# Gate blocks copied to DRAM in runs of 16 KB, the first three copies of a set issued late, and 48 parked score blocks in place of 44

## The chip, the cores and the metric

The kernel runs on one core of one Trainium2 chip. The time is the device time of one execution in microseconds (us). TensorE (PE) multiplies matrices, VectorE (DVE) and ScalarE (ACT) work elementwise, GpSimd (POOL) issues the gathers of single rows here, SyncE (SP) issues most loads. DMA queues started by SP, ACT and POOL share 16 DMA engines.

## The reference

One decoder layer on 512 tokens of width 2048: attention and a recurrent branch, then a retrieval layer with 16384 experts of one neuron each. The change touches only the last part:

```python
s1 = jnp.einsum('chd,hnd->chn', q[:, :, 0], keys1); s2 = ...   # 8 heads, 128 keys each
v1, i1 = lax.top_k(s1, 16); v2, i2 = lax.top_k(s2, 16)
top, pos = lax.top_k(v1[..., :, None] + v2[..., None, :], 16)  # 16 of 256 pairs
e = i1[pos // 16] * 128 + i2[pos % 16]                         # expert numbers
g = jax.nn.softmax(top, axis=-1)
act = jax.nn.gelu(einsum('chkd,cd->chk', u_tab[e], x))
out = einsum('chk,chkd->cd', g * act, v_tab[e])
```

## The kernel before

The first 960 us or so (projections, attention, recurrent branch, output projection, queries and the choice of the top 16) are untouched. Then the retrieval layer splits the tokens. For the first 160 tokens the rows of the two expert tables are gathered one by one: one row for each token (1 MB) per gather, started by POOL (`gather`, L932) into one of a few row buffers, and one product on DVE (L953, L959 or L965) per gather. One such product with its gather is a **side step** (`side`); there are 320. For the other 352 tokens (`TD`) the kernel computes the scores of all experts densely, in 128 **blocks** of 128 experts.

One block is an **S job**: two halves of weights (`ud`), each loaded by SP into a `raw` buffer (L135; both halves are one load of 1 MB), split by ACT into a rounded part `hi` (L152) and by DVE into a rest `lo` (L153), and multiplied by PE in 48 matmuls (L197 to L199, 24 for each half). Four pairs of `hi` and `lo` exist. The result goes through Gelu (L753 or L1130) and is multiplied by the block's **gate** matrix `G`. Four blocks make a group; the output products of a group are four **V jobs** (48 matmuls each, L1154 to L1156).

The gates come from one-hot products. DVE makes one-hot matrices for four tokens at a time (`onehots`, L998 to L1001), PE multiplies them (12 small matmuls, `gate_mm`, L1014), ACT copies the result from PSUM into the staging tile `stg` (L1016). After eight such steps, a **set** of 32 tokens, `stg` holds 2 MB and ACT starts its copy to the DRAM tensor `GD` (L1019). There are 11 sets and one `stg`, so the first copy of a set waits until the transfer of the set before has landed. To give PE work in this **gate stage** (about 960 to 1333 us), S jobs are done early and **parked**: `park` computes a block, applies Gelu and stores it to DRAM (`AD`, L754). 44 blocks are parked, ten of them before the gate stage, three in each set (steps 0, 3 and 6) and one after the last set. 16 side steps are done in this stage, on two row buffers (`rowA` and `acc`).

In the **main stage** the remaining 84 S jobs alternate with V jobs, in an order written out by hand (`manual_schedule`); the gates of a group are read back by one transfer of 704 KB (`gates`, L1050), one group ahead, into one of two buffers. After each half of a job `pace` adds `RATE` to a debt and does a side step whenever it reaches 1. In the **tail** the parked blocks come back (`fetch`, L1090), meet their gates, and only V jobs remain; there the rate is 0.4 per half.

In the gate stage the order on each engine is not the program's order: a scheduler takes each instruction as soon as it thinks it ready, in program order among those. In that stage each engine runs its own list strictly in order, so an instruction that waits holds up everything behind it on its engine. The few lines that matter:

```python
GD = dr.tile([NCH, NBLK // GRP, 128, GRP * 32], F32, name="GD")        # L730
s.activation(stg[0][:, :, qq * 4:(qq + 1) * 4].rearrange("p a t -> p t a"), ...)   # L1016
s.dma_start(GD[q // 8].rearrange("g p x -> p g x"), ...)               # L1019
if q % 8 in (0, 3, 6):
    park()
sy.dma_start(G.rearrange("p c a t -> p c (a t)"), GD[:, gi].rearrange("c p x -> p c x"))   # L1050
```

Of the kernel before, what the change touches and what calls it, by code (L numbers as in the profile page):

```python
# [7 lines left out]
F32 = mybir.dt.float32  # L8
# [4 lines left out]
AF = mybir.ActivationFunctionType  # L13
# [9 lines left out]
NBLK = 128  # L23
GRP = 4
# [2 lines left out]
EB = 2  # L27
TG = 128 + TX
TD = S - TG
PARK = 44  # L30


C_MIX, C_QN, C_KVN, C_QHN, C_QHR, C_KHN, C_KHR = 0, 16, 20, 22, 23, 24, 25
# [8 lines left out]
def body(tc, nc, d, dbg=None):  # L42
    v, s, g, pe, sy = nc.vector, nc.scalar, nc.gpsimd, nc.tensor, nc.sync
# [20 lines left out]
    def bank():  # L64
        return pp.tile([128, 512], F32, name="ps")
# [32 lines left out]
    groups += [([("wq", m, 0), ("wq", m, 1)], d["wq"][m]) for m in range(16)]  # L98
    JOBS = [("S", b) for b in range(PARK)]
    for gi in range(PARK // GRP, NBLK // GRP + 1):  # L100
        for i in range(GRP):
            if gi < NBLK // GRP:
                JOBS.append(("S", gi * GRP + i))
            if gi > PARK // GRP:
                JOBS.append(("V", gi - 1, i))
    for gi in range(PARK // GRP):
        for i in range(4):
# [212 lines left out]
    xc, ga, gi, th = (sl[:, 8 + 2 * i:10 + 2 * i, :] for i in range(4))  # L320
# [178 lines left out]
    for hb in range(2):  # L499
# [3 lines left out]
        for t in range(NTT):  # L503
            ts = slice(t * 128, (t + 1) * 128)
            ps = bank()
# [28 lines left out]
        for u in range(3):  # L534
            hi, lo = need("wuq", hb, u)
            for m in range(2):
                ps = bank()
# [21 lines left out]
        for m in range(4):  # L559
            ps = bank()  # L560
# [20 lines left out]
        for i in range(4):  # L581
            ps = bank()
            pe.matmul(ps, ident[:8, 4 + i:5 + i].to_broadcast([8, 128]), rr[:8], start=True, stop=True)
            v.tensor_tensor(kn[i], kn[i], ps, op=OP.mult)
        for j in range(2):
            ps = bank()
# [6 lines left out]
        for i in range(4):  # L593
# [6 lines left out]
            for b in range(NTT):  # L600
                n = (b + 1) * 128
                qs = slice(b * 128, (b + 1) * 128)
                ps = bank()
# [71 lines left out]
    dr = pool("dr", space=DRAM)  # L675
# [22 lines left out]
    for k in range(KT):  # L698
        ps = bank()
# [14 lines left out]
    for k in range(KT):  # L714
        ps = bank()
# [11 lines left out]


    NCH = TD // 32
    GD = dr.tile([NCH, NBLK // GRP, 128, GRP * 32], F32, name="GD")  # L730
    AD = dr.tile([PARK, 128, TD], F32, name="AD")
    pkp = pool("park")

# [10 lines left out]
    def park():  # L744

        b = parked[0]
        if b >= PARK:
            return
        parked[0] += 1
        ps = bank()  # L750
        s_matmuls(b, ps[:, :TD])
        a = pkp.tile([128, TD], F32, name="pact", bufs=2)
        s.activation(a, ps[:, :TD], AF.Gelu)  # L753
        s.dma_start(AD[b], a)  # L754
# [43 lines left out]
    for m in range(16):  # L798
        ps = bank()
# [100 lines left out]
    for i in range(len(SLOTS)):  # L900
        if i < NG0:
            c = "AB"
        elif i < U1:
            c = "ABCY" if i < U1 - 4 else "ABC"
        elif i < V0:
            c = "ABCX" if i < V0 - 4 else "ACX"
        elif i < V1:
            c = "ACXY" if i < V1 - 4 else "ACY"
        else:
            c = "ACY"  # L910
        if i in (U1, V0):
            used_at["X" if i == U1 else "Y"] = i + 0.5
        p = min(c, key=lambda p: used_at.get(p, -1))
# [87 lines left out]
            v.tensor_tensor(o3[:, j], o1, g3T[:, j, c, None].to_broadcast(sh), op=OP.mult)  # L1001
        oh[q] = (o2.rearrange("p t a b -> p t (a b)"), o3.rearrange("p j t a b -> p j t (a b)"))

    stg = [None]

    def gate_mm(q):

        o2, o1 = oh.pop(q)
        if q % 8 == 0:
            stg[0] = gp.tile([128, 128, 32], F32, name="stg", bufs=1)  # L1010
        ps = bank()
        for i in range(4):
            for j in range(3):
                pe.matmul(ps[:, i * 128:(i + 1) * 128], o2[:, i], o1[:, j, i], start=j == 0, stop=j == 2)  # L1014
        qq = q % 8
        s.activation(stg[0][:, :, qq * 4:(qq + 1) * 4].rearrange("p a t -> p t a"),  # L1016
                     ps.rearrange("p (t a) -> p t a", t=4), AF.Copy)
        if qq == 7:
            s.dma_start(GD[q // 8].rearrange("g p x -> p g x"), stg[0].rearrange("p (g a) t -> p g (a t)", a=GRP))  # L1019

    for q in range(2):
        onehots(q)
    for q in range(NB4):
        if q % 8 in (0, 3, 6):
            park()
        if q % 8 == 0 or q % 16 == 11:
            side()
        if q + 2 < NB4:
            onehots(q + 2)
        gate_mm(q)  # L1030
# [12 lines left out]
    def wide():  # L1043
        return pp.tile([128, EB, 512], F32, name="pw")
# [2 lines left out]
    Pt, Gt, At = {}, {}, {}  # L1047
    def gates(gi):
        G = ep.tile([128, NCH, GRP, 32], F32, name="G", bufs=2)
        sy.dma_start(G.rearrange("p c a t -> p c (a t)"), GD[:, gi].rearrange("c p x -> p c x"))  # L1050
        Gt[gi] = G

    pcnt = [0]
# [25 lines left out]
    def pace(x):  # L1079
        debt[0] += x  # L1080
        while debt[0] >= 1:
            debt[0] -= 1
            side()
# [20 lines left out]

    vs = [j[1] for j in JOBS if j[0] == "V" and j[2] == 0]
    vnext = dict(zip(vs, vs[1:]))
    RATE = 0.81
    for ji in range(PARK, len(JOBS)):
        job = JOBS[ji]
        if job[0] == "S":  # L1110
# [3 lines left out]
            ps = wide()[:, 0, :TD]  # L1114
            for hf in range(2):
# [9 lines left out]
                post = []  # L1125
                pace(RATE)

# [5 lines left out]
        else:  # L1133
            _, gi, dc = job

            gn = vnext.get(gi)
            tail = gn is not None and gn < PARK // GRP
# [10 lines left out]
            for pr in range(2):  # L1148
                hi, lo = need("vd", gi, dc, pr)
                for i in range(4):  # L1150
                    for bj in range(2):
                        ph, pl = Pt[gi * GRP + 2 * pr + bj]
                        ws = slice(bj * 512 + i * 128, bj * 512 + (i + 1) * 128)
                        pe.matmul(pss[i], hi[:, ws], ph, start=pr + bj == 0, stop=False)  # L1154
                        pe.matmul(pss[i], lo[:, ws], ph, start=False, stop=False)  # L1155
                        pe.matmul(pss[i], hi[:, ws], pl, start=False, stop=pr + bj == 2)  # L1156
                for f in post:
                    f()
                post = []
                if tail and pr == 1:  # L1160
                    b = gn * GRP + dc
                    gated(At.pop(b), b)
                pace(0.4 if tail else RATE)

            def fin(pws=pws, dc=dc, gi=gi):
                for i, pw in enumerate(pws):
# [16 lines left out]
    for dc in range(4):  # L1183
        ps = wide()[:, 0]
# [85 lines left out]
```

## Time and profile before

| | |
|---|---|
| three runs | 3004.95, 3007.82, 3014.71 us; median 3007.82 |
| profiled execution | 3004.65 us; span of its instructions 3002.6 us |
| PE busy | 2916.7 us, 97% of the span |
| DVE, ACT, POOL busy | 2370.0, 1079.6, 581.7 us |
| DMA | 756.68 MB, 252 GB/s over the span |
| chain of waits, by engine | PE 64%, DVE 12%, issue 9%, DMA 7% |

A matmul's end is modelled and matmuls overlap, so PE's idle time says more than its busy time. The granted clock is a mean over a stretch; 1.00 is the upper of its two levels (2.4 GHz), 0.50 the lower (1.2 GHz). Most of what matters here lies between 950 and 1340 us and is read there, stretch by stretch.

### The profile page before, as it was taken

The numbers are of one execution on the slowest core, as the hardware profiler recorded it, in microseconds if no ns is written. First come the engines' busy times: TensorE is split into PE (matmuls) and PEld (weight loads), VectorE is DVE, ScalarE is ACT, GpSimd is POOL, SyncE is SP. The second block draws the span as 40 slices with busy tenths as digits, with TensorE's granted clock in tenths as the row PEclk, the third lists the DMA queues.
The fourth block names the chain that finished last, engine by engine and source line by source line (L and its number), as shares of the span: only waits on it lengthen the run. The fifth ranks groups of instructions, "written<-read, shape, count | busy, mean of one in ns | idle before, by whom it ended". The sixth has DMA issues, their size and how long they took to land.

```text
span 3002.6 us, 41808 instructions
## 1 busy us (share of the span) xinstructions
PE 2916.7 (97%) x16987; PEld 2682.0 (89%) x16987; DVE 2370.0 (79%) x3391; ACT 1079.6 (36%) x1390; POOL 581.7 (19%) x350
## 2 busy tenths in 40 slices
PE   8999999999998889999999999999999999999999
PEld 6777565778888789999999999999999999999998
DVE  4376544447999866659999998999999999988886
ACT  4346332442224335443333333333323333323332
POOL 0000000000001100003333333333334343311110
PEclk9999898999999899999999999999999999999999
DMA  7222211223226765679999999999999999987874
GB/s 242 89 88 77 91 51 43 96 92 113 84 94 218 268 208 185 193 236 386 377 381 364 374 356 349 382 354 371 362 366 366 370 370 371 374 296 286 294 283 180
DMA packets 204991, 756.68 MB, mean 252 GB/s; under 512 B 13824, under 2 KB 116800, under 8 KB 123008
## 3 DMA queue, kind: packets, MB, share of 16 engines
q1 hardware_dynamic: 105072, 381.42, 35.1%
q0 software_dynamic: 46560, 338.71, 29.0%
q10 hardware_dynamic: 53168, 33.89, 3.6%
q8 instruction: 133, 2.18, 0.3%
q14 instruction: 58, 0.48, 0.0%
HBM read 717.04 MB, written 36.93 MB: 251 GB/s over the span
## 4 chain that ended last, share of the span: by engine, by line
PE 64%; DVE 12%; issue 9%; DMA 7%; POOL 4%; ACT 3%; POOLq 0%; ACTq 0%; DVEq 0%; SPq 0%
PE ps L197 7%; PE ps L199 7%; PE ps L198 7%; PE pw L1154 6%; PE pw L1155 6%; PE pw L1156 6%; PE pw L197 4%; PE pw L199 4%; PE pw L198 4%; DVE acc L959 3%; DVE lo L153 3%; DMA raw<-in_vd 2%; DMA GD<-stg 2%; PE ps L446 2%; PE ps L448 2%
## 5 line engine op out<-in xcount | busy, mean ns | idle before, releaser
L152 ACT ACTIVATE hi<-raw 128x1024 fp32r<-128x1024 f32 x631 | 657.9, 1056 | 1078.6 <-PE ps L198 346.0
L153 DVE TENSOR_TENSOR lo<-raw,hi 128x1024 fp32r<-128x1024 f32 x631 | 768.4, 1221 | 311.0 <-ACT hi L152 296.0
L1154 PE MATMUL pw<-FH,hi 128*128 128x352 f32 x1536 | 499.7, 325 | 9.8 <-DVE acc L1168 5.6
L1155 PE MATMUL pw<-FH,lo 128*128 128x352 f32 x1536 | 499.0, 325 | 0.0
L1156 PE MATMUL pw<-FL,hi 128*128 128x352 f32 x1536 | 498.9, 325 | 0.0
L197 PE MATMUL pw<-FH,hi 128*128 128x352 f32 x1344 | 435.2, 324 | 0.6 <-ACT pact L753 0.6
L199 PE MATMUL pw<-FH,lo 128*128 128x352 f32 x1344 | 434.2, 323 | 0.0
L198 PE MATMUL pw<-FL,hi 128*128 128x352 f32 x1344 | 433.0, 322 | 0.0
L199 PE MATMUL ps<-FH,lo 128*128 128x352 f32 (+1 forms) x960 | 330.8, 345 | 4.7 <-DVE lo L153 4.7
L197 PE MATMUL ps<-FH,hi 128*128 128x352 f32 (+1 forms) x960 | 335.2, 349 | 0.0
L198 PE MATMUL ps<-FL,hi 128*128 128x352 f32 (+1 forms) x960 | 330.7, 345 | 0.0
L1154 PEld LDWEIGHTS pw<-FH,hi 128*128 128x128 f32 x1536 | 290.3, 189 | 11.7 <-issue 6.9
L1156 PEld LDWEIGHTS pw<-FL,hi 128*128 128x128 f32 x1536 | 290.2, 189 | 0.0
L1155 PEld LDWEIGHTS pw<-FH,lo 128*128 128x128 f32 x1536 | 290.2, 189 | 0.0
L198 PEld LDWEIGHTS pw<-FL,hi 128*128 128x128 f32 x1344 | 254.3, 189 | 0.0
L197 PEld LDWEIGHTS pw<-FH,hi 128*128 128x128 f32 x1344 | 253.0, 188 | 0.9 <-ACT pact L753 0.9
L199 PEld LDWEIGHTS pw<-FH,lo 128*128 128x128 f32 x1344 | 252.0, 187 | 0.0
L1168 DVE TENSOR_TENSOR acc<-pw,acc 128x704 f32<-128x704 f32 x256 | 215.5, 883 | 8.4 <-PE pw L1156 8.4
L199 PEld LDWEIGHTS ps<-FH,lo 128*128 128x128 f32 x960 | 182.6, 190 | 16.3 <-DVE lo L153 5.6
L197 PEld LDWEIGHTS ps<-FH,hi 128*128 128x128 f32 x960 | 182.9, 191 | 14.5 <-issue 4.4
L198 PEld LDWEIGHTS ps<-FL,hi 128*128 128x128 f32 x960 | 183.1, 191 | 10.1
L1155 PE MATMUL pw<-ph,lo 128*128 128x352 f32 x512 | 165.4, 323 | 0.0
(330 smaller groups left out, 4912.3 us busy)
## 6 DMA issues: line engine op xcount, KB each, us to landing
raw<-in_ud SPq DMA_DIRECT2D x128, 1024.0 KB, 5.9
raw<-in_vd SPq DMA_DIRECT2D x128, 1024.0 KB, 6.0
G<-GD SPq DMA_DIRECT2D x33, 704.0 KB, 9.8
GD<-stg ACTq DMA_DIRECT2D x11, 2048.0 KB, 12.2
raw<-in_win SPq DMA_DIRECT2D x20, 1024.0 KB, 4.8
raw<-in_wo SPq DMA_DIRECT2D x16, 1024.0 KB, 4.8
raw<-in_wq SPq DMA_DIRECT2D x16, 1024.0 KB, 4.8
AD<-pact ACTq DMA_DIRECT2D x44, 176.0 KB, 2.0
```

The costliest lines, as they stand in the source:

```text
L152: s.activation(hi, raw, AF.Copy)
L153: v.tensor_tensor(lo, raw, hi.bitcast(F32), op=OP.subtract)
L197: pe.matmul(out, ah, bh, start=start, stop=False)
L198: pe.matmul(out, ah, bl, start=False, stop=False)
L199: pe.matmul(out, al, bh, start=False, stop=stop)
L446: pe.matmul(pss[t], mh_, wh, start=cc == 0, stop=False)
L448: pe.matmul(pss[t], ml_, wh, start=False, stop=cc == 7)
L959: v.scalar_tensor_tensor(acc[:, 0, :], r, W0[:, j:j + 1], acc[:, 0, :], op0=OP.mult, op1=OP.add)
L1154: pe.matmul(pss[i], hi[:, ws], ph, start=pr + bj == 0, stop=False)
L1155: pe.matmul(pss[i], lo[:, ws], ph, start=False, stop=False)
L1156: pe.matmul(pss[i], hi[:, ws], pl, start=False, stop=pr + bj == 2)
L1168: v.tensor_tensor(a, pw[:, :, :TD], a, op=OP.add)
```

## The change

Four edits. `GD` is laid out so that a partition's part of a set is one run of 16 KB in place of 32 runs of 512 bytes; the reads of a group's gates keep their runs of 512 bytes, which now lie 16 KB apart in DRAM and lay side by side before. The copies of a set's steps 0, 1 and 2 are held and issued at step 3, behind the park there. 48 blocks are parked: five parks are added, at steps 0, 2, 8, 16 and 24 of the stage, and the one after the last set falls away. The side steps' rates go from 0.81 to 0.82, and from 0.4 to 0.45 in the tail, which now has 12 groups in place of 11.

```diff
-PARK = 44
+PARK = 48
...
-    GD = dr.tile([NCH, NBLK // GRP, 128, GRP * 32], F32, name="GD")
+    GD = dr.tile([NCH, 128, NBLK * 32], F32, name="GD")
...
-    stg = [None]
+    stg, held = [None], []
...
         qq = q % 8
-        s.activation(stg[0][:, :, qq * 4:(qq + 1) * 4].rearrange("p a t -> p t a"),
-                     ps.rearrange("p (t a) -> p t a", t=4), AF.Copy)
+
+        def copy(st=stg[0]):
+            s.activation(st[:, :, qq * 4:(qq + 1) * 4].rearrange("p a t -> p t a"),
+                         ps.rearrange("p (t a) -> p t a", t=4), AF.Copy)
+        if qq < 3:
+            held.append(copy)
+            return
+        for f in held:
+            f()
+        held.clear()
+        copy()
         if qq == 7:
-            s.dma_start(GD[q // 8].rearrange("g p x -> p g x"), stg[0].rearrange("p (g a) t -> p g (a t)", a=GRP))
+            s.dma_start(GD[q // 8], stg[0].rearrange("p a t -> p (a t)"))
...
         if q % 8 in (0, 3, 6):
             park()
+        if q in (0, 2, 8, 16, 24):
+            park()
...
-        sy.dma_start(G.rearrange("p c a t -> p c (a t)"), GD[:, gi].rearrange("c p x -> p c x"))
+        gw = GRP * 32
+        sy.dma_start(G.rearrange("p c a t -> p c (a t)"),
+                     GD[:, :, gi * gw:(gi + 1) * gw].rearrange("c p x -> p c x"))
...
-    RATE = 0.81
+    RATE = 0.82
...
-                pace(0.4 if tail else RATE)
+                pace(0.45 if tail else RATE)
```

How the order on the engines moves is seen at three places. The first is ACT at the start of the second set, from the transfer of the first set on (`hi` is a split, `pact` a park's Gelu, `stg` a gate copy, `AD` a park's store). Before:

```order
L1019 DMA GD<-stg 128x32x128
L152 ACTIVATE hi<-raw 128x1024
L753 ACTIVATE pact<-ps 128x352
L152 ACTIVATE hi<-raw 128x1024
L754 DMA AD<-pact 128x352
L1016 ACTIVATE stg<-ps 128x4x128 x3
L152 ACTIVATE hi<-raw 128x1024 x2
```

Now:

```order
L1028 DMA GD<-stg 128x4096
L152 ACTIVATE hi<-raw 128x1024
L753 ACTIVATE pact<-ps 128x352
L152 ACTIVATE hi<-raw 128x1024
L754 DMA AD<-pact 128x352
L152 ACTIVATE hi<-raw 128x1024 x2
L753 ACTIVATE pact<-ps 128x352
L1018 ACTIVATE stg<-ps 128x4x128
```

Two more splits and one more park stand between the transfer and the first copy of the next set. So it is in the sets that begin at steps 8, 16 and 24, which have a park more.

The second place is ACT in the sets from step 32 on. Now:

```order
L1028 DMA GD<-stg 128x4096
L152 ACTIVATE hi<-raw 128x1024
L753 ACTIVATE pact<-ps 128x352
L152 ACTIVATE hi<-raw 128x1024
L754 DMA AD<-pact 128x352
L1018 ACTIVATE stg<-ps 128x4x128 x3
L152 ACTIVATE hi<-raw 128x1024 x2
```

This is the order that all sets had before: the scheduler takes the three held copies at the same place as ever.

The third place is DVE in the second set (`rowA` and `acc` in L953 are side steps, `o_` are one-hots, `lo` is a split that PE waits for). Before:

```order
L153 TENSOR_TENSOR lo<-raw,hi 128x1024
L1001 TENSOR_TENSOR o_7199<-o_7198,g3T 128x512 x3
L998 TENSOR_TENSOR o_7284<-iox,e2T 128x512
L999 TENSOR_TENSOR o_7285<-iox,e1T 128x512
L953 SCALAR_TENSOR_TENSOR rowA,dots<-rowA,xg 128x2048
L1001 TENSOR_TENSOR o_7286<-o_7285,g3T 128x512 x3
L953 SCALAR_TENSOR_TENSOR acc,dots<-acc,xg 128x2048
L153 TENSOR_TENSOR lo<-raw,hi 128x1024
```

Now:

```order
L999 TENSOR_TENSOR o_7471<-iox,e1T 128x512
L953 SCALAR_TENSOR_TENSOR rowA,dots<-rowA,xg 128x2048
L1001 TENSOR_TENSOR o_7472<-o_7471,g3T 128x512 x3
L953 SCALAR_TENSOR_TENSOR acc,dots<-acc,xg 128x2048
L153 TENSOR_TENSOR lo<-raw,hi 128x1024 x2
L999 TENSOR_TENSOR o_7493<-iox,e1T 128x512
L153 TENSOR_TENSOR lo<-raw,hi 128x1024
L953 SCALAR_TENSOR_TENSOR rowA,dots<-rowA,xg 128x2048
L953 SCALAR_TENSOR_TENSOR acc,dots<-acc,xg 128x2048
```

Four side steps, two on each row buffer, stand close together here, and three splits stand between them.

## Rows read from the trace of the kernel before

**Rows 1.** Stretches: length; busy PE, PEld, DVE, ACT, POOL; PE clock, DMA share, GB/s.

```profile
950.00:985.00 35.00, 24.08 (x145) 22.13 (x144) 32.48 (x58) 9.07 (x13) 7.10 (x5) 0.76 0.65 238
...
1010.00:1035.00 25.00, 12.10 (x85) 11.29 (x84) 14.20 (x31) 7.81 (x9) 1.25 (x2) 0.73 0.63 221
...
1058.00:1080.00 22.00, 11.79 (x84) 10.98 (x83) 12.20 (x25) 8.88 (x10) 0.94 (x1) 0.77 0.45 155
1080.00:1330.00 250.00, 242.05 (x1990) 236.86 (x1989) 169.63 (x368) 123.99 (x141) 0.00 (x0) 0.99 0.60 191
```

**Rows 2.** Waits, 860 to 1340 us: total, times, longest.

```profile
PE ps L1014 <- DVE o L1001: 40.4, 13, 12.9
...
ACT stg L1016 <- DMA GD<-stg: 58.4, 8, 14.8
```

**Rows 3.** ACT in order of time, start of the second set.

```profile
999.18 0.38 ACTq L1019 DMA_DIRECT2D GD<-stg  x1
...
1005.80 5.37 ACTq L754 DMA_DIRECT2D AD<-pact  x1
1021.50 2.73 ACT L1016 ACTIVATE stg<-ps 128x512 f32<-128x512 f32 x3 [14.78 <-DMA GD<-stg]
```

**Rows 4.** Stretches after the first two stalls, columns as in rows 1.

```profile
965.00:980.00 15.00, 9.59 (x54) 8.37 (x53) 12.96 (x25) 3.21 (x3) 3.79 (x2) 0.52 0.75 279
1029.00:1035.00 6.00, 5.72 (x29) 5.21 (x30) 6.00 (x16) 1.09 (x1) 0.94 (x1) 0.57 0.72 197
```

**Rows 5.** A stretch of the main stage, columns as in rows 1.

```profile
1500.00:1800.00 300.00, 300.00 (x1868) 300.00 (x1867) 279.52 (x285) 98.72 (x117) 106.32 (x64) 1.00 0.96 369
```

**Rows 6.** DMA issues (count, KB, us to landing): 960 to 1080, 1080 to 1330, whole run.

```profile
GD<-stg ACTq DMA_DIRECT2D x2, 2048.0 KB, 20.7
...
GD<-stg ACTq DMA_DIRECT2D x9, 2048.0 KB, 11.9
...
out<-acc POOLq DMA_DIRECT2D x1, 1024.0 KB, 5.6
```

**Rows 7.** Start of the gate stage: Gelu of a park (ACT), next split (DVE).

```profile
959.86 0.46 ACT L753 ACTIVATE pact<-ps 128x352 f32<-128x352 f32 x1 [2.40 <-PE ps L199]
...
962.19 1.22 DVE L153 TENSOR_TENSOR lo<-raw,hi 128x1024 fp32r<-128x1024 f32 x1
```

**Rows 8.** ACT in order of time, start of a later set.

```profile
1143.69 0.42 ACTq L1019 DMA_DIRECT2D GD<-stg  x1
...
1156.48 2.98 ACT L1016 ACTIVATE stg<-ps 128x512 f32<-128x512 f32 x3 [5.65 <-DMA GD<-stg]
```

**Rows 9.** A gather on the chain, and DVE where the next one is waited for.

```profile
974.44 7.99 DMA rowA<-in_un,E
...
992.34 2.29 DVE L953 SCALAR_TENSOR_TENSOR rowA<-rowA,xg 128x2048 f32<-128x2048 f32 x1 [0.15 <-DMA rowA<-in_un,E]
```

**Rows 10.** Groups by line, 1080 to 1330 us: busy, mean ns, idle before.

```profile
L1001 DVE TENSOR_TENSOR o<-o,g3T 128x512 bf16<-128x512 bf16 x192 | 70.6, 420 | 0.8
...
L153 DVE TENSOR_TENSOR lo<-raw,hi 128x1024 fp32r<-128x1024 f32 x50 | 61.0, 1221 | 33.4 <-ACT hi L152 29.6 <-PE ps L1014 3.8
```

**Rows 11.** Start of the main stage: ACT's last gate transfer, DVE's first gated block.

```profile
1325.98 0.38 ACTq L1019 DMA_DIRECT2D GD<-stg  x1
...
1342.99 0.53 DVE L1059 TENSOR_TENSOR pact<-pact,G 128x352 f32<-128x352 f32 x1 [0.16 <-DMA G<-GD]
```

**Rows 12.** Main stage, 1400 to 2600 us: queues (packets, MB, share) and DMA issues.

```profile
q0 software_dynamic: 36421, 264.84, 56.3%
q1 hardware_dynamic: 49254, 175.34, 39.1%
...
raw<-in_vd SPq DMA_DIRECT2D x79, 1024.0 KB, 6.7
raw<-in_ud SPq DMA_DIRECT2D x76, 1024.0 KB, 6.8
G<-GD SPq DMA_DIRECT2D x19, 704.0 KB, 13.0
```

## The prediction

> **What bounds the kernel now.** I read the page first: PE is busy for 97% of the span, so the kernel is bound by PE nearly everywhere and only the stretches where PE stands still can be won. Its table of slices has low PE digits, apart from the first one, in slices 13 to 15, so the view by stretches came next. It shows three holes in the gate stage and a thin loss after them [rows 1]. In 950 to 985 us PE is idle for 35.0 - 24.1 = 10.9 us, in 1010 to 1035 for 12.9, in 1058 to 1080 for 10.2, and in the 250 us after that for 8.0 in all; 42.0 us together. PEclk, third from the right, says that a hole is paid twice: after it the clock is granted at its lower level for some time.
>
> The waits say what ends the holes [rows 2]: PE waits 40.4 us for one-hots of DVE, and ACT 58.4 us for the transfer `GD<-stg`. The list of ACT shows how the second makes the first [rows 3]. The transfer of the first set starts at 999.18; ACT then comes to the first gate copy of the next set, whose `stg` is still being read, and stands for 14.78 us, until 1021.50. The splits `hi` behind that copy are late, DVE's `lo` and the one-hots behind them too, and PE runs out of weights. A reader should see that PE never waits for the transfer itself: it waits for what stands behind the waiting copy on ACT, which runs strictly in order.
>
> The clock's price: from 965 to 980 us PE is busy for 9.59 us at a mean of 0.52, so 0.96 of it at the lower level, and half of that, 4.6 us, is lost; from 1029 to 1035 us it is 5.72 us at 0.57, a loss of 2.5 [rows 4]. The third hole looks like the second, 2.5 more; in the 250 us at 0.99 there are about 5 us at the lower level, 2 us lost. The clock takes 11.6 us. So **idle time and clock in the gate stage are worth 42.0 + 11.6 = 53.6 us**, and the rest of the kernel offers hardly anything.
>
> **The change part by part.**
>
> *Late copies and further parks.* These are one edit in effect. In the sets from steps 8, 16 and 24 the first copy now stands behind a second park and two more splits. A block is 48 matmuls; in the main stage 1868 matmuls fill 300 us [rows 5], so a block is 7.7 us. The copy is thus reached some 2 x 7.7 = 15.4 us after the transfer starts, where it was reached after 7. Even at the 20.7 us that the first two transfers took [rows 6] the wait is 5 us and no longer 14.8, and the splits of the next two halves are already made, which is PE's work for 7.7 us. The second and third hole lose their cause. From step 32 on, ACT's order has not moved at all, so there only a faster transfer helps.
>
> The first hole has another cause: the one-hots of the first set stand behind side steps. The two parks at steps 0 and 2 put PE work before the first small matmuls. What stays is the wait for the first of those parks: PE's block ends about 959.5 (Gelu starts at 959.86), and the `lo` that the next one needs ends at 962.19 + 1.22 = 963.4 [rows 7]. I keep 3.9 us idle, with bounds of 2 (ACT's order brings that split earlier) and 10.9 (nothing gained).
>
> *Runs of 16 KB.* Later sets wait 12.8 us from the transfer's start to the first copy, 5.65 of them idle [rows 8]. No row shows a write of 2 MB in long runs. The nearest are the same 2 MB in short runs, 11.9 us, and a write of 1 MB in runs of 8 KB, 5.6 us [rows 6]; between them and near the middle I take 9 us. At anything below 11 ACT's next splits come 1 to 3 us sooner, and the 1 us that each set loses (8.0 over eight) goes; I keep 1 us in all, bounds 0 and 10 (with the clock).
>
> The Trainium skill (DMA: Bandwidth & Descriptors, Specifications) sets 512 bytes as the least transfer for line rate, by which the short runs would be no slower than the long ones. The rows speak against it, mildly: 2 MB in 11.9 us is 176 GB/s, and the 1 MB write in long runs reached 187. By that rule the second rival below would hold.
>
> *DVE in the new order.* Now PE no longer stands still, and DVE comes up. A side step is 2.29 us and its gather lands 8 us after the buffer is free [rows 9], so with two buffers a pair cannot recur faster than in 10.3 us. I walked DVE's new list from 962.2 on with a split at 1.22, three one-hot products at 1.1 (1.26 at most) [rows 10] and that gather time, and PE's list beside it with 7.7 us per block and 0.7 per gate step. The worst place is the third of the orders shown. A product on `rowA` ends at 998, its next row lands at 1006; product to 1008.4, one-hots to 1009.5, product on `acc` to 1011.8, split to 1013. PE has used up its halves at 1008.7: idle for 4.5 us. Four smaller places (before the second half of the third park, at the fourth set's one-hots, twice in the third set) give 0.7, 0.5, 1.2 and 2.3. Sum 9.2 us, bounds 2 (gathers land as early as the scheduler thought) and 20 (each place doubled). The holes of 3.9 and 4.5 us may each drop the clock; at 2.3 each that is 4.6.
>
> Left in the gate stage: 3.9 + 9.2 + 4.6 + 1 = 18.7. **Recovered: 53.6 - 18.7 = 34.9 us.**
>
> *Blocks moved.* Four blocks leave the main stage and enter the gate stage: 4 x 7.7 us of PE work on either side, no sum. Their stores and loads, 176 KB each, run beside it; the cover is DMA that stands at 0.60 in the gate stage [rows 1].
>
> *Start of the main stage.* The park after the last transfer is gone, so the first main block takes its place, and its gates are wanted one block sooner. Today the transfer starts at 1325.98 and the first gated product follows at 1342.99, 17.0 us later, having waited 0.16 for `G` [rows 11]. Now DVE reaches it about 8 us after the transfer and holds for some 6 to 9 us. Three halves are split ahead, 11.6 us of PE work, and the split behind the gated product is due at about 21 us. I take 1 us, bounds 0 and 5.
>
> *Rates.* 304 side steps remain after the 16 of the gate stage. With 312 halves at 0.82, 96 at 0.45 and 8 at 0.82 the last falls due one half before the end, where there were four halves to spare; its product (2.3 us) has 3.9 us of cover. In full swing the main stage has PE at 300.00 of 300, DVE at 279.5, DMA at 0.96 [rows 5]. 0.01 more per half is 1.2% of the side steps, 0.6% of DVE and 0.7% of DMA, inside the room of 7% and 4%. I take 0, bounds 0 and 0.6% of 1240 us = 7.
>
> **Sum.** 3004.65 - 34.9 + 1 = 2970.8 us for the profiled execution. It lies 3.2 us below the median of the three runs and at their lowest; I forecast **2972 us**. A measurement of this kernel tells about 0.3%, 9 us, from no change.
>
> **The rivals.**
>
> *The gathers keep up.* For it: in 950 to 1058 DVE waited for gathers seldom and for 0.15 us in the row shown [rows 9]. Against it: two products on each buffer now stand within nine instructions. Left are 3.9 + 2 + 2.3 + 1: recovered 44.4, **2961 us**. Chance 0.22.
>
> *Long runs are no faster.* The transfers stay at 11.9 and 20.7 us. The holes still go, by order alone; the thin loss of 8 + 2 us stays, 9 more than forecast: **2981 us**. For it, the 5.6 us for 1 MB, which doubled is 11.2 [rows 6]. Chance 0.14.
>
> *The gate reads become dear*, the rival on the other side. The 1408 runs of a read now lie 16 KB apart; before, the 128 of each set filled one stretch of 64 KB. Place: the main stage, where DMA stands at 0.96 [rows 5]. In 1400 to 2600 us [rows 12] the gathers' 36421 packets take 56.3% of 16 x 1200 us, 297 ns each for 7.3 KB; 155 loads of 128 packets of 8 KB at the same rate take 6630 of the 7507 us of q1, so the 26752 packets of 19 gate reads take some 877 us, 33 ns each, and one read 2.9 us of all engines. A read comes every 8 blocks, 61.7 us, with 4% or 2.5 us free. So up to 5.4 us a read costs nothing; beyond, 20 reads pay the excess. At 7.1 us (2.45 times) the whole gain is gone; at three times, 8.7 us, 66 us are lost: **3037 us**. For it: nothing in this trace has that pattern. Against it: 13.0 us from issue to landing [rows 12] against a use some 50 us later, so latency alone is covered. Chance 0.09.
>
> The Trainium skill (DMA: Bandwidth & Descriptors, Latency and other measured facts) reports copies that lose a quarter to half of their rate when rows lie 2 MiB or more apart, at powers of two, and proposes to pad the pitch. 16 KB is far below what it lists, and no run here shows such a pitch; if the loss began so low, this rival would hold.
>
> *The added rate tips DVE or the start of the main stage stalls*, both at their bounds: 7 + 5 on top of the forecast, 2983 us. Chance 0.07.
>
> **How the numbers follow.** The forecast, 2960 to 2985 with the bounds of its own terms, has 0.48. The rivals at 2961, 2981 and 2983 make 0.43 more on the faster side, though a tail of 0.04 of these ends within 0.3% where several bounds meet. Slower comes from the dear reads alone: 0.09. So faster 0.87, same 0.04, slower 0.09. For 8 in 10 the range leaves out the dear reads and a little of each end: 2953 to 2992.
>
> **What would show it.** Right: no stretch in 985 to 1080 with PE idle for 10 us; `ACT stg <- DMA GD<-stg` below 10 us in total; `GD<-stg` landing in 8 to 11 us; PE's remaining waits in the first two sets for `lo` or one-hots with DVE waiting for `rowA` or `acc`; main stage with PE as full as before. Wrong: `GD<-stg` unchanged and the thin loss with it; `G<-GD` landing in 20 us or more, DMA at 1.0 and PE idle on `hi` or `lo` in the main stage; or DVE waits in the second and third set above 20 us, which would mean that the gathers were mis-sized.

## The result and the profile after

| | before | after |
|---|---|---|
| median, us | 3006.39 (4 runs, 3004.56 to 3014.71) | 2969.53 (4 runs, 2966.67 to 2975.53) |
| profiled execution, us | 3004.65 | 2966.67 |
| its span, us | 3002.6 | 2964.5 |

The ratio is 0.9872, with a 95% interval of 0.9855 to 0.989: 1.3% faster. The forecast was 2972 us, and 2970.8 for the profiled execution.

The first view to read is again the one by stretches. The same four stretches as in [rows 1], and the two behind them, where the main stage begins (columns as in [rows 1]):

```profile
950.00:985.00 35.00, 34.13 (x236) 33.17 (x236) 34.65 (x59) 13.91 (x18) 4.24 (x4) 1.00 0.68 252
1010.00:1035.00 25.00, 19.65 (x154) 18.31 (x153) 23.68 (x38) 10.82 (x12) 4.49 (x4) 0.86 0.91 341
1058.00:1080.00 22.00, 22.00 (x199) 21.69 (x197) 18.01 (x40) 14.24 (x17) 0.00 (x0) 1.00 0.49 180
1080.00:1330.00 250.00, 248.21 (x2036) 244.89 (x2035) 173.12 (x365) 127.11 (x143) 0.00 (x0) 1.00 0.55 204
1330.00:1350.00 20.00, 16.91 (x97) 16.63 (x96) 8.99 (x11) 3.90 (x6) 7.10 (x6) 0.91 0.96 354
1350.00:1400.00 50.00, 49.08 (x305) 48.72 (x305) 46.66 (x48) 16.80 (x23) 16.30 (x11) 1.00 0.99 395
```

The first hole is down from 10.9 us of idle PE to 0.9, the second from 12.9 to 5.35, the third is gone, and the thin loss is down from 8.0 to 1.8, all of it behind 1300 us, where the last set ends. A new small one stands at 1330 to 1350. The granted clock, third from the right, is below 1.00 only behind the two holes that are left.

The waits from 860 to 1370 us, to be held against [rows 2] (total, times, longest):

```profile
DVE pact L1072 <- DMA G<-GD: 6.8, 1, 6.8
...
ACT stg L1018 <- DMA GD<-stg: 19.4, 7, 3.7
...
PE ps L1014 <- DVE o L1001: 5.7, 3, 3.6
...
DVE acc L953 <- DMA acc<-in_un,E: 4.5, 2, 3.9
```

PE's wait for one-hots fell from 40.4 to 5.7 us. ACT still waits for the gate transfer in seven sets, but never longer than 3.7 us, where it had been 14.8. The next view says why, for the second set: ACT in order of time, to be read against [rows 3].

```profile
999.79 0.33 ACTq L1028 DMA_DIRECT2D GD<-stg  x1
...
1006.25 1.05 ACT L152 ACTIVATE hi<-raw 128x1024 fp32r<-128x1024 f32 x1
1006.38 0.33 ACTq L754 DMA_DIRECT2D AD<-pact  x1
1014.56 2.01 ACT L152 ACTIVATE hi<-raw 128x1024 fp32r<-128x1024 f32 x2 [7.26 <-DMA raw<-in_ud]
1016.48 0.44 ACT L753 ACTIVATE pact<-ps 128x352 f32<-128x352 f32 x1
1016.82 1.14 ACT L1018 ACTIVATE stg<-ps 128x512 f32<-128x512 f32 x1
```

The first gate copy comes 17.0 us after the transfer's start and waits for nothing. But ACT waits at 1014.56 in its turn: for the load of the next weights, issued at 1001.6, which took 12.9 us beside the 2 MB transfer and two gathers. PE does not feel this wait; the list of DVE further down shows why. The DMA issues (count, KB, us to landing) from 960 to 1080 us and from 1080 to 1330 us, to be held against [rows 6]:

```profile
GD<-stg ACTq DMA_DIRECT2D x2, 2048.0 KB, 14.7
...
GD<-stg ACTq DMA_DIRECT2D x9, 2048.0 KB, 9.9
```

### The profile page after: what moved, and what is told of

Same layout as the page of the kernel before. It is cut to its first block, busy times and chain, and to the rows that moved or that the text cites. A ratio compares the mean times of both kernels' runs of the same rounds, so it can differ in the third digit from the quotient of the medians.

```text
span 2964.5 us, 41822 instructions
## 1 busy us (share of the span) xinstructions
PE 2907.1 (98%) x16987; PEld 2673.7 (90%) x16987; DVE 2367.7 (80%) x3391; ACT 1077.0 (36%) x1390; POOL 562.0 (19%) x350
## 4 chain that ended last, share of the span: by engine, by line
PE 64%; DVE 11%; issue 10%; DMA 8%; POOL 4%; ACT 2%; SPq 0%; POOLq 0%; ACTq 0%; DVEq 0%
PE ps L197 8%; PE ps L199 8%; PE ps L198 8%; PE pw L1167 7%; PE pw L1168 7%; PE pw L1169 7%; DVE lo L153 3%; DMA raw<-in_vd 3%; PE pw L197 3%; PE pw L199 3%; PE pw L198 3%; PE ps L446 2%; DVE acc L959 2%; PE ps L447 2%; PE ps L448 2%
## 5 line engine op out<-in xcount | busy, mean ns | idle before, releaser
L1167 PE MATMUL pw<-FH,hi 128*128 128x352 f32 x1536 | 499.6, 325 | 10.2 <-DVE acc L1181 7.0
L1168 PE MATMUL pw<-FH,lo 128*128 128x352 f32 x1536 | 498.7, 325 | 0.8 <-DVE lo L153 0.8
L1169 PE MATMUL pw<-FL,hi 128*128 128x352 f32 x1536 | 498.5, 325 | 0.0
L199 PE MATMUL pw<-FH,lo 128*128 128x352 f32 x1280 | 414.4, 324 | 3.1 <-DVE lo L153 3.1
L197 PE MATMUL pw<-FH,hi 128*128 128x352 f32 x1280 | 415.2, 324 | 1.8 <-ACT stg L1018 1.8
L198 PE MATMUL pw<-FL,hi 128*128 128x352 f32 x1280 | 413.1, 323 | 0.0
L199 PE MATMUL ps<-FH,lo 128*128 128x352 f32 (+1 forms) x1024 | 348.9, 341 | 4.9 <-DVE lo L153 4.9
L197 PE MATMUL ps<-FH,hi 128*128 128x352 f32 (+1 forms) x1024 | 353.3, 345 | 0.0
L198 PE MATMUL ps<-FL,hi 128*128 128x352 f32 (+1 forms) x1024 | 348.7, 341 | 0.0
L1167 PEld LDWEIGHTS pw<-FH,hi 128*128 128x128 f32 x1536 | 289.8, 189 | 13.4 <-issue 9.2
L1168 PEld LDWEIGHTS pw<-FH,lo 128*128 128x128 f32 x1536 | 289.8, 189 | 1.1 <-DVE lo L153 1.1
L1169 PEld LDWEIGHTS pw<-FL,hi 128*128 128x128 f32 x1536 | 289.9, 189 | 0.0
L199 PEld LDWEIGHTS pw<-FH,lo 128*128 128x128 f32 x1280 | 240.5, 188 | 3.4 <-DVE lo L153 3.4
L197 PEld LDWEIGHTS pw<-FH,hi 128*128 128x128 f32 x1280 | 241.5, 189 | 2.0 <-ACT stg L1018 2.0
L198 PEld LDWEIGHTS pw<-FL,hi 128*128 128x128 f32 x1280 | 242.7, 190 | 0.0
L199 PEld LDWEIGHTS ps<-FH,lo 128*128 128x128 f32 x1024 | 192.8, 188 | 16.4 <-DVE lo L153 5.7
```

The costliest lines, as they stand in the source:

```text
L197: pe.matmul(out, ah, bh, start=start, stop=False)
L198: pe.matmul(out, ah, bl, start=False, stop=False)
L199: pe.matmul(out, al, bh, start=False, stop=stop)
```

## The experiments

Each kernel was timed in five rounds beside the kernel before. The ratios are to that.

**Without the late copies.**

```diff
-        if qq < 3:
+        if False:
             held.append(copy)
```

> The changed kernel without its late copies: every copy is issued at its own step. In the lists of all five engines nothing moves against the changed kernel, since the scheduler puts the held copies where it would have put them anyway. Theory: the late copies are no part of the gain; 2970 us, within 5 us of the changed kernel, one copy still reached some 15 us after the transfer's start in sets 2 to 4. Rival (holding matters through the PSUM banks or the order of buffers): 2980 us or more, ACT stg <- DMA GD<-stg above 40 us.

Measured: 2971.16 us, ratio 0.9879 (0.9856 to 0.9901); `ACT stg <- DMA GD<-stg` 19.9 us in place of 19.4. The late copies are no part of the gain. In program order they move; in the lists that the engines run nothing does. The prediction had noted this for the sets from step 32 on and did not see that it holds for all. What delays the first copy of sets 2 to 4 is the further park alone.

**The layout alone, and the parks alone.** The first of these kernels is the kernel before with only the new layout (the lines that write and read `GD` follow it as in the change):

```diff
-    GD = dr.tile([NCH, NBLK // GRP, 128, GRP * 32], F32, name="GD")
+    GD = dr.tile([NCH, 128, NBLK * 32], F32, name="GD")
```

> The kernel before with the new layout alone; order as before. Theory: GD lands in 15 us in the first two sets and 10 later, so ACT's stand at the second and third set falls from 15 to 9 us each and the thin loss of 10 us goes; the first hole of 11 us stays. Saved 6 + 6 + 10 = 22 us: 2984 us, between 2979 and 2991. Rival A (order alone): no more than 8 us saved, 2998 us or more. Rival B (layout carries the gain): below 2976 us.

The second is the changed kernel with the same edit the other way round:

> The changed kernel with the old layout of GD, runs of 512 bytes both written and read; order on all engines as in the changed kernel. Theory of the prediction (long runs are worth the thin loss, 9 to 10 us): 2977 us, between 2974 and 2982, GD landing in 20 us in the first two sets and 12 in the others. Rival A (the order alone does it, the transfer is hidden): 2970 us, within 3 us of the changed kernel. Rival B (the layout carries the gain): above 2985 us with waits of ACT for GD above 60 us.

| | old layout | new layout |
|---|---|---|
| 44 parks | 3007.76 us | 2991.33 us, 0.9939 (0.9919 to 0.9958) |
| 48 parks | 2981.87 us, 0.9911 (0.9893 to 0.9928) | 2969.53 us, 0.9872 |

Neither carries the gain alone: the parks give 26 us without the layout and 22 with it, the layout 16 without the parks and 12 with them. (48 parks here means with the new rates and the copies held, both of which cost and give nothing that these runs can tell.) The 2969.53 us are from another series than the other three; the kernel without the late copies, which runs the same lists and was timed beside those three, has 2971.16, and with it the last two figures are 20 and 11. The last step, 11 to 12 us, is somewhat more than the 9 by which the rival of short runs had been priced. Its time alone hardly shows it, since the intervals of these two kernels overlap (0.9893 to 0.9928 and 0.9856 to 0.9901). The stretch that shows it is the one from 1080 to 1300 us; with the parks and the old layout, and then in the changed kernel, it reads

```profile
1080.00:1300.00 220.00, 214.48 (x1765) 210.14 (x1763) 151.79 (x328) 108.86 (x125) 0.00 (x0) 1.00 0.60 193
```

```profile
1080.00:1300.00 220.00, 220.00 (x1822) 217.11 (x1821) 156.68 (x339) 112.56 (x127) 0.00 (x0) 1.00 0.55 206
```

PE is idle for 5.5 us in the first and for nothing in the second; the two profiled executions, 2974.61 and 2966.67 us, are 8 us apart. The DMA issues of the kernel with short runs, from 960 to 1080 and from 1080 to 1340 us, are close to those of [rows 6]:

```profile
GD<-stg ACTq DMA_DIRECT2D x2, 2048.0 KB, 22.2
...
GD<-stg ACTq DMA_DIRECT2D x9, 2048.0 KB, 12.0
```

The layout alone lies 0.3 us beyond the slow end of its expected range. Its second and third hole, in the order of the kernel before, shrink to 5.9 and 6.5 us:

```profile
1010.00:1035.00 25.00, 19.13 (x129) 17.15 (x127) 19.33 (x38) 9.57 (x11) 3.51 (x3) 0.73 0.78 294
...
1058.00:1080.00 22.00, 15.51 (x119) 14.58 (x118) 15.97 (x31) 10.44 (x13) 1.68 (x1) 0.84 0.38 138
```

The clock column tells what was not counted: the second hole is halved, and the clock of its stretch is 0.73, no better than in [rows 1]. With the parks and the old layout PE is busy for 19.12 us of the same 25, at 0.86. So for the second hole either half of the change does nearly all that both do (19.65); what the changed kernel has left there has another cause, below.

**Which park fills which hole.** Two kernels keep a part of the five parks and put the others behind the last set.

```diff
-        if q in (0, 2, 8, 16, 24):
+        if q in (0, 2):
```

> The changed kernel with the further parks at steps 0 and 2 alone; the three others stand behind the last set. Theory (each park takes away the hole of its own set): the first hole of 10.9 us and its clock of 4.6 go, the second and third sets keep what the run with the new layout alone shows, 5.9 and 6.5 us idle with their clock of some 4, and the start of the main stage is full. From 2991 us of the layout alone, 14 us less: 2977 us, between 2973 and 2981. Rival A (the parks at 0 and 2 shift the work of the later sets too, so that these need no park): 2968 us, with less than 3 us idle between 1035 and 1100. Rival B (the first hole only moves): above 2985 us.

Measured: 2974.35 us, ratio 0.9884 (0.9864 to 0.9904).

```diff
-        if q in (0, 2, 8, 16, 24):
+        if q in (8, 16, 24):
```

> The changed kernel with the further parks at steps 8, 16 and 24 alone; the two others stand behind the last set. Theory: the first hole (10.9 us idle before 985, clock at 0.76 in 950 to 985) is as in the kernel before, all else as in the changed kernel, and 4 us less at the start of the main stage: 2970 + 14 - 4 = 2980 us, between 2976 and 2984. Rival A (the first hole is filled by any earlier park): 2970 us. Rival B (a gate stage that starts late loses more behind it): above 2986 us.

Measured: 2983.53 us, ratio 0.9922 (0.9907 to 0.9937). The first hole, in the kernel with the later parks and then in the one with the first parks:

```profile
950.00:985.00 35.00, 24.10 (x150) 22.25 (x149) 32.88 (x61) 11.98 (x19) 6.15 (x4) 0.80 0.65 238
```

```profile
950.00:985.00 35.00, 34.36 (x238) 33.55 (x237) 34.63 (x62) 14.07 (x19) 4.24 (x4) 1.00 0.66 244
```

The first hole goes with the parks at 0 and 2 and with no other. Without the three later ones PE is idle for 6.3 us from 1035 to 1080, as expected and where the changed kernel has nothing; the 5.8 us of the second set are hardly more than the changed kernel's 5.35, so the park at step 8 does little there beside the new layout. The parks at steps 0 and 2 are worth the most: without them the time is 14 us above the changed kernel, without the three others 5 us, both already with what a park behind the last set gives back. The 14 us are clear of the intervals, the 5 us are not.

**The park behind the last set.**

```diff
-        if q in (0, 2, 8, 16, 24):
+        if q in (0, 2, 8, 16):
```

> The changed kernel without the further park of the fourth set (step 24), which stands behind the last set instead, as one did in the kernel before. Theory: PE's holes at the start of the main stage in the changed kernel (1.8 us at the last set's end, 3.1 us at 1340 to 1350, with the clock some 6 us) come from the missing park, since the first gates are wanted one block sooner; a park there takes 4 to 6 of them away, and the fourth set's first copy, reached some 7 us after its transfer starts, waits 3 us with no more than 1 us of it felt by PE: 2965 us, 3 to 5 us below the changed kernel. Rival A (the hole is made by DVE's gathers, not by the wait for G): no change within 2 us. Rival B (the fourth set needs its park): 2975 us with a hole of 5 us or more near the fourth set.

Measured: 2967.0 us, ratio 0.9861 (0.984 to 0.9882). The interval overlaps that of the changed kernel, so the time does not tell them apart; the stretch does. In this kernel the main stage starts full, at the full clock:

```profile
1330.00:1350.00 20.00, 20.00 (x128) 20.00 (x127) 12.24 (x13) 4.08 (x8) 6.43 (x5) 1.00 1.03 399
```

against 16.91 us and 0.91 in the changed kernel. From 1300 to 1400 us PE is idle for 1.1 us here and for 5.8 in the changed kernel. DVE's wait for `G` is down from 6.8 to 1.4 us. The fourth set does without its park: from 1080 to 1300 us PE is idle for 0.1 us.

**No side steps in the gate stage.**

```diff
-        if q % 8 == 0 or q % 16 == 11:
-            side()
...
-    RATE = 0.82
+    RATE = 0.86
...
-                pace(0.45 if tail else RATE)
+                pace(0.48 if tail else RATE)
```

> The changed kernel with no side step in the gate stage; all 320 are done in the main stage, at 0.86 and 0.48 for each half. Asks for two things. One: is the hole left in the second set (5.3 us idle in 1010 to 1035) made by side steps? Theory: yes, the one-hots stand behind products that wait for gathers while the first transfer fills the DMA engines; without them PE is idle for less than 1.5 us from 985 to 1300. Rival: the split waits for its weights' load behind the transfer; 3 us or more stay. Two: has the main stage room for 5% more side steps? Theory: the rows give DVE 93% and DMA 96 to 97% there, so 4.9% more steps bring DMA by 2.7% to 0.99 or 1.00, at the edge: PE loses 0 to 15 us in 1400 to 2700, total 2965 to 2985 us. Rival: the room is there, no loss, 2962 us.

Measured: 3000.95 us, ratio 0.9964 (0.995 to 0.9979). The two questions have answers in the stretches; the profiled execution, 3009.88 us, is the slowest of this kernel's nine:

```profile
1010.00:1035.00 25.00, 25.00 (x204) 24.74 (x203) 15.15 (x32) 12.26 (x15) 0.00 (x0) 1.00 0.54 194
...
1400.00:1900.00 500.00, 492.25 (x3039) 491.11 (x3038) 465.17 (x470) 150.85 (x188) 180.05 (x110) 0.99 0.98 378
1900.00:2400.00 500.00, 484.22 (x2958) 481.57 (x2957) 462.28 (x396) 154.42 (x190) 184.46 (x112) 0.99 0.95 368
```

The hole of the second set is made by side steps: without them PE is busy throughout. And the main stage has no room for 5% more: PE loses 7.8 and 15.8 us in the two stretches of 500 us, against 3.1 and 3.6 in the changed kernel, and the time is 31 us above it (28 above the run with the old rate, below, of the same series), although the second set gave back some 8 (5.6 idle and 2.8 of the clock). So the main stage and its start pay 36 to 40 us, 2.3 to 2.5 us for each of the 16 side steps. The expected 0 to 15 us was too little. Whether DVE or DMA is what runs out there was not separated: DVE is busy for 465.2 and 462.3 us of these stretches, hardly other than in the changed kernel (463.9 and 463.9).

**The rates.**

```diff
-    RATE = 0.82
+    RATE = 0.81
...
-                pace(0.45 if tail else RATE)
+                pace(0.48 if tail else RATE)
```

> The changed kernel with the old rate 0.81 in full swing and 0.48 in the tail, so that the last side steps still fall before the end. Theory: the rate of 0.82 costs nothing, 2970 us within 3 us. Rival: it costs the 3 us by which PE stands more in 1400 to 2600, then 2967 us or less and PE idle below 3 us in 1400 to 2400; or the tail has no room for 0.48, then above 2974 us with PE below 97% in 2400 to 2900.

Measured: 2973.14 us, ratio 0.9892 (0.9872 to 0.9912). From 1400 to 2900 us PE is idle for 8.0 us here, and for 9.8 and 7.9 in two executions of the changed kernel: nothing to tell apart, and the ratios overlap. As far as these runs tell, the 0.01 is free, as predicted.

**The changed kernel once more,** beside the run that follows.

> The changed kernel itself, timed beside the run before it on the same chip: 2970 us within 3 us.

Measured: 2972.7 us, ratio 0.9877 (0.9858 to 0.9897).

**Side steps kept out of the first sets.** Moving the calls alone was not tried; the trace says that it would hardly do, since the 16 calls of the changed kernel stand at steps 0 to 80, and yet the scheduler has all their gathers started before 1050 us (POOL has no work from 1058 to 1330 in the first view). So two kernels give it a reason to wait. The first holds the gathers.

```diff
+    def place_tile(p):
+        return home[p]
...
-        if q in (0, 2, 8, 16, 24):
+        if q in (0, 2, 8, 16):
...
-        if q % 8 == 0 or q % 16 == 11:
+        if q % 4 == 0 and 20 <= q <= 80:
+            for p in freed:
+                v.tensor_copy(place_tile(p)[:, 0:1], oh[q + 1][0][:, 0, 0:1])
             side()
```

> The changed kernel with two edits: the further park of step 24 behind the last set, and the 16 side steps spread over steps 20 to 80, one each fourth step, each held at its place: before its gather, DVE writes one column of the row buffer from the one-hots of that step, so the gather can't be issued earlier. Theory from the runs so far: the hole of the second set (5.3 us, and its clock, 1 to 3) goes as it does without side steps, the main stage starts full as with the park behind the last set, and its rate is that of the changed kernel: 2961 us, between 2956 and 2965, 8 to 10 us below the changed kernel. Rival A (the gathers, later, disturb the later sets): a hole of 2 us or more for some of the sets from 1080 on, 2967 us or above. Rival B (a side step slips into the main stage): 2966 us with DVE rows late at its start.

Measured: 3024.5 us, ratio 1.0058 (1.0037 to 1.0079): over 60 us beside what was expected, and slower than before. The six runs spread from 3008.21 to 3034.34 us, and the profiled one is the fastest of them, so what the slower ones lost beyond it is not seen. The hole of the second set is indeed gone, but the later sets pay. The wait that came, and the stretch in which it stands:

```profile
DVE rowA L953 <- DMA rowA<-in_un,E: 76.7, 7, 11.7
```

```profile
1080.00:1300.00 220.00, 193.40 (x1391) 181.80 (x1389) 151.71 (x312) 91.27 (x100) 12.88 (x12) 0.87 0.56 209
```

DVE stood seven times for 11 us before a product whose gather had just been let go, and one-hots and splits stood behind it. Over these 220 us PE was idle for 26.6 us, and the clock cost another 0.13 x 193.4 = 25. So the next kernel holds the product and not the gather (edit against the kernel just above):

```diff
-    def place_tile(p):
-        return home[p]
...
         if q % 4 == 0 and 20 <= q <= 80:
-            for p in freed:
-                v.tensor_copy(place_tile(p)[:, 0:1], oh[q + 1][0][:, 0, 0:1])
+            j = SLOTS[ng[1]][2]
+            v.tensor_copy(dots[:, j:j + 1], oh[q + 1][0][:, 0, 0:1])
             side()
```

> As the run before (the further park of step 24 behind the last set, 16 side steps at each fourth step from 20 to 80), but now the product is held and not the gather: before it, DVE writes the column of its sums from the one-hots of that step. So a gather is issued as soon as its buffer is read, some two side steps or 30 us ahead of its own product. Theory: what the run before lost (77 us of DVE waiting for rowA) came of products that stood right behind their gathers; with 30 us of lead that wait is gone, PE is idle for less than 4 us from 960 to 1300, and the time is 2961 us, between 2955 and 2966. Rival: side steps in the later sets hold up the one-hots by themselves (2.3 us each, with copies at each step), then PE is idle for 10 us or more from 1080 to 1300 and the time is above 2972 us.

Measured: 2954.89 us, ratio 0.9827 (0.9811 to 0.9842), which lies below the intervals of the changed kernel: **a version that beats both**, by 1.7% and by 15 to 18 us, and just under its expected range. It holds two edits: the park of step 24 behind the last set alone gave 2967.0 us, so by the medians the side steps' new places are worth the other 12. The second set is full, at the full clock, and PE's wait for one-hots is 0.2 us:

```profile
1010.00:1035.00 25.00, 25.00 (x220) 24.61 (x219) 17.57 (x39) 13.55 (x16) 0.00 (x0) 1.00 0.38 141
...
1080.00:1300.00 220.00, 219.66 (x1843) 216.41 (x1841) 192.04 (x393) 117.05 (x131) 12.18 (x13) 1.00 0.71 267
```

```profile
PE ps L1014 <- DVE o L1001: 0.2, 1, 0.2
```

DVE does more from 1080 to 1300 us than in the changed kernel (192.0 us busy, there 156.7), and DMA goes from 0.55 to 0.71: the side steps now stand where both have room. The start of the main stage is not full in this kernel: from 1330 to 1350 us PE is busy for 17.30 us, and DVE waits 10.7 us for `G`.

## Why the prediction was right, step by step

The total was right to some 4 us, and part of that is luck: two errors cancel. The gate stage recovered 7.6 us more than forecast, and the start of the main stage cost 4 us more. The profiled execution gained 38.0 us. The terms, from the stretches (idle PE, and busy time times what is missing of the clock):

| term | predicted, us | measured, us |
|---|---|---|
| left: first wait | 3.9 | 35.0 - 34.13 = 0.9 |
| left: DVE and gathers, 985 to 1080 | 9.2 | 0.2 + 5.35 = 5.6 |
| left: clock | 4.6 | 0.14 x 19.65 = 2.8 |
| left: thin loss, 1080 to 1330 | 1 | 250.0 - 248.21 = 1.8 |
| recovered | 53.6 - 18.7 = 34.9 | 53.6 - 11.1 = 42.5 |
| start of the main stage, 1330 to 1400 | 1 | 4.0 + 1.5 - 0.55 = 5.0 |
| main stage, 1400 to 2900 | 0 | 9.8 - 9.4 = 0.4 |
| gain | 33.9 | 37.1 |

The start is idle PE and clock of the two stretches from 1330 to 1400 us, less the 0.55 us idle there before. The 53.6 us took the clock from short stretches behind the holes. By whole stretches, as in the measured column, the clock of the kernel before costs 14.2 us and not 11.6, and the gain adds up to 39.7; so the sum closes to some 2 us and no better.

*Late copies and further parks.* The mechanism holds, with two corrections: the parks do it, and the late copies nothing; and in the second set the new layout alone shrinks the hole as far as the parks do. One sign was missed: `ACT stg <- DMA GD<-stg` was to fall below 10 us in total and stands at 19.4. It was the wrong sign, since all seven waits lie behind 1080 us, and up to 1300 us PE loses nothing by them.

The first wait, 3.9 us with a lower bound of 2, was a misreading. It was taken from [rows 7], from a split that ends at 963.4 and that the second park was thought to need. But DVE makes two other splits before that one, in the kernel before and in the changed one:

```profile
955.86 2.35 DVE L153 TENSOR_TENSOR lo<-raw,hi 128x1024 fp32r<-128x1024 f32 x2
```

```profile
956.44 2.35 DVE L153 TENSOR_TENSOR lo<-raw,hi 128x1024 fp32r<-128x1024 f32 x2
```

So PE had both halves of its next block by 958.8 and goes on without a gap when the first park ends, about 960.4. The 0.9 us left in this stretch are 0.21 for a split at 956.37 and 0.65 for one-hots at 969.00.

*Runs of 16 KB.* 9 us was taken, between 5.6 and 11.9, and 9.9 measured in the steady sets (14.7 in the first two, for which no figure was forecast). The thin loss went as forecast: from 1080 to 1300 us nothing is left of it. The 1.8 us stand at the end of the last set, where a park had stood before; with one put back behind that set PE is idle for 0.55 us from 1300 to 1330. The rule that made the rival of short runs, in the Trainium skill (DMA: Bandwidth & Descriptors, Specifications), is that 512 bytes already give line rate; the trace disagrees, with 12.0 us against 9.9 for the same 2 MB, and the kernel with short runs took 2981.87 us where the rival had 2981 (in part luck: the rival priced the short runs at 9 us, and 11 to 12 were measured). Another section of that page of the Trainium skill (DMA: Bandwidth & Descriptors, Why small descriptors are slow) counts three bus cycles for each packet beside one for every 32 bytes; by that 512 bytes take 19 cycles in place of 16, an estimate of 1.19, and the trace agrees in the time to landing with 12.0 / 9.9 = 1.21. It does not in the time that the packets of ACT's queue took: from 1080 to 1330 us that is 27.3% of 16 engines for 21.38 MB in the kernel before and 22.8% for 23.43 MB in the changed one, parks' stores included, 1.31 times as much for each byte. So what makes short runs slower stays open.

*DVE in the new order.* The place and the cause were right: in the second set, products on `rowA` and `acc` that wait for gathers, and one-hots and splits behind them. DVE in order of time shows it:

```profile
1005.34 1.14 DVE L1001 TENSOR_TENSOR o<-o,g3T 128x512 bf16<-128x512 bf16 x3
1010.38 2.29 DVE L953 SCALAR_TENSOR_TENSOR acc<-acc,xg 128x2048 f32<-128x2048 f32 x1 [3.90 <-DMA acc<-in_un,E]
...
1015.65 1.23 DVE L153 TENSOR_TENSOR lo<-raw,hi 128x1024 fp32r<-128x1024 f32 x1 [0.37 <-ACT hi L152]
1016.80 2.28 DVE L953 SCALAR_TENSOR_TENSOR rowA<-rowA,xg 128x2048 f32<-128x2048 f32 x1
...
1019.66 2.29 DVE L953 SCALAR_TENSOR_TENSOR acc<-acc,xg 128x2048 f32<-128x2048 f32 x1 [0.57 <-DMA acc<-in_un,E]
...
1022.22 1.14 DVE L1001 TENSOR_TENSOR o<-o,g3T 128x512 bf16<-128x512 bf16 x3
```

DVE makes no one-hots ready for PE from 1006.5 to 1022.2 (4.5 us of it are waits for gathers and 6.9 the three products) and has its own arrears to work off behind that. The rival for this hole, the late load of weights on which ACT stood until 1014.56, costs DVE 0.37 us. PE still has matmuls until 1024 and then stands for one-hots twice, 5.1 us:

```profile
1025.56 1.38 PE L1014 MATMUL ps<-o,o 128*128 128x128 bf16 x12 [1.43 <-DVE o L1001]
1030.58 0.27 PE L1014 MATMUL ps<-o,o 128*128 128x128 bf16 x1 [3.64 <-DVE o L1001]
```

So the worst place cost 5.1 us where 4.5 were taken, some 15 us later than in the walk. What failed is the four smaller places: 4.7 us were taken for them and next to nothing came. Gathers from 985 to 1060 us land after a median of 6.8 us on `rowA` and 8.5 on `acc`, where 8 was taken from one row of the chain [rows 9]. Those beside a transfer took longest: 11.4 us (`acc`, which made the 3.90 above) and 10.3 beside the first, 12.9 beside the second. In the four other executions with this order in these sets the loss from 985 to 1080 is 5.0, 5.4, 5.6 and 8.0 us. The rival in which the gathers keep up would have had 2 us here.

*Start of the main stage.* This is the step that failed in the other direction: 1 us with a bound of 5, and 5.0 measured (3.0, 4.3 and 4.7 in three other executions with the same order there). The forecast had the cause (DVE holds for `G`, for 6 to 9 us) but let three splits cover it. DVE at that place:

```profile
1335.12 0.53 DVE L1072 TENSOR_TENSOR pact<-pact,G 128x352 f32<-128x352 f32 x1 [6.83 <-DMA G<-GD]
1336.22 0.52 DVE L1087 TENSOR_TENSOR FL<-pact,FH 128x352 fp32r<-128x352 f32 x1 [0.56 <-ACT FH L1084]
1341.28 2.29 DVE L953 SCALAR_TENSOR_TENSOR rowC<-rowC,xg 128x2048 f32<-128x2048 f32 x1 [4.54 <-DMA rowC<-in_un,E]
1343.50 1.22 DVE L153 TENSOR_TENSOR lo<-raw,hi 128x1024 fp32r<-128x1024 f32 x1
```

`G` came 17.0 us after the transfer's start, exactly as in [rows 11]. But behind it stood a second wait, 4.54 us for the first row in a new buffer, ahead of the split. That wait was queued on DVE and had not been counted. The gather for that row could not start earlier: POOL's wait for the new buffer ended at 1330.1, when the last gate transfer had landed (11.9 us after 1318.1).

*Rates and blocks moved.* Free, as said.

*The dear gate reads* did not come. From 1400 to 2600 us, the queue and the reads of the changed kernel, and then of the one with 48 parks and the old layout:

```profile
q1 hardware_dynamic: 53398, 178.29, 39.9%
...
G<-GD SPq DMA_DIRECT2D x21, 704.0 KB, 12.3
```

```profile
q1 hardware_dynamic: 53473, 179.25, 39.9%
...
G<-GD SPq DMA_DIRECT2D x21, 704.0 KB, 12.1
```

About as many packets take the same share with a pitch of 16 KB as with the runs side by side.

## What to carry to other kernels

A hole that is filled in one place shows the next cause, so the walk through every engine's new list is worth its trouble, and it has to include the second wait behind the first. Edits in program order may do nothing where a scheduler re-orders, as the late copies here did: read the engines' lists before a price is put on them, and give the scheduler a dependence if an instruction is to stay late. When something is held, hold the consumer and let its load go early.

## What had not been expected of the hardware

The run length does more than set the rate. In the kernel before, the issue of a park's store on ACT's own queue, behind a transfer in short runs, lasted up to 9.84 us (5.37 in [rows 3]), and up to 9.01 in the kernel with 48 parks and short runs; with runs of 16 KB all 34 issues from 990 to 1340 us took 0.33 us, and so did all 33 with the layout alone. In the steady sets that issue (2.9 us) ends before the copy's wait does, so there it costs nothing of its own; whether the longer ones of the second and third set did was not tried.

The main stage stands at an edge: with DMA at 0.96 to 0.98, 1.2% more side steps were free, and 5% more cost 2.3 to 2.5 us each, about the 2.3 us of a product.

In the first two sets, where gathers run beside it, a transfer of 2 MB in short runs took 22.2 us in place of 12.0 in the later sets; in long runs it took 14.7 in place of 9.9. That the gathers make the difference was not tried by itself.
